# Order of the expert quads in a one-core hybrid SSD / convolution / hierarchical-MoE block

## The chip, the core and the metric

The kernel runs on one core of a Trainium2 chip. The metric is the device time of one execution in microseconds; of several executions the median is given.

## What is computed

One decoder layer over 512 tokens of width 1024: a gated SSD branch and a causal convolution branch, an output projection, then a hierarchical mixture of experts, a gate from per-layer embeddings and a final norm. The change touches the mixture of experts alone. Cut to that, the reference is:

```python
g_idx = argmax(u @ wg + bg)                      # one group of 4 for each token
top_v, top_i = top_k(e_logits[g_idx], 2)         # two of the 8 experts in it
gate_w = softmax(top_v) * g_prob
hdn = silu(xb @ w_gate[e]) * (xb @ w_up[e])      # for each of 32 experts e, on its tokens
out[token] += (hdn @ w_down[e]) * gate_w
```

Each expert has three float32 matrices of 1024x512 or 512x1024, 2 MiB each. All 32 experts are computed, so 192 MiB of expert weights are read in every execution.

## The kernel before

**Slots and quads.** The 32 experts are put into 32 slots. A slot holds 32, 64 or 96 tokens; the most loaded experts get the widest slots (NFIX and RANK, lines 51 to 67; the first four slots belong to experts 0 to 3, whatever their load). A quad is four strips of 32 tokens, 128 in all: "22" is a quad of two experts with two strips each, "31" two experts with three strips and one, "211" three experts. PLAN (line 52) lists the quads, one string for each group; a group of two quads shares a dispatch and a combine. Tokens over a slot's width would be handled by a loop behind the groups (line 1704), as often as the routing of the tokens needs.

**Units.** Each quad makes six units (lines 1351 to 1369): four of `gu_unit` (gate and up, two halves each) and two of `d_unit`. A unit multiplies 32 times: on each of 32 steps one strip of tokens (128x32, the stationary operand) against 512 columns of that strip's expert weights. So every unit has 32 matmuls, in whatever way the four strips fall to experts. A unit loads one piece of 1 MiB for each expert of its quad (lines 1209 and 1222): two pieces in a "22" or "31" quad, three in a "211" quad.

**The weight queue.** `pump` (lines 270 to 283) issues the loads in the order of the units on SP's queue, while there is room: ten pages of 1 MiB hold expert pieces. When a unit's matmuls have been issued, its pages are given back (line 369), and on the chip the next loads wait until TensorE has finished with them. For the experts behind the first four, SP first reads the expert's number (line 1182), which the router has worked out.

**Other work of TensorE between the units.** `step` runs one unit and `after` (lines 341 to 353) then inserts tasks: `disp` (line 1280, gathers the tokens of the next group by one-hot matmuls, four tasks for each group), `back` (line 1286, one for each quad) and `combine` (line 1317, adds the outputs of the group before to the tokens, eight for each group). What decides is a credit: a unit adds 1.27 for each half MiB that it loaded less 3.5 of its own, up to 5; a task takes its cost off; tasks go in while the credit is above zero, or once their due unit is reached (`task`, lines 1364, 1377, 1383). A hidden-layer step stands between a quad's fourth and fifth unit (`hid_act`, `hid_mul`, `hid_tr`, lines 1224 to 1241). `hot` (line 1248) builds the one-hot tables of the next group on VectorE, one instruction for each expert.

In the rows, `w<-eg`, `w<-eu` and `w<-ed` are the loads of gate, up and down weights; `acc<-w,cj` is a matmul of a gate or up unit, `acc<-w,m` of a down unit, `acc<-w,uh` and `acc<-w,ul` of `disp`, `acc<-identr,w` and `acc<-cb,w` of `back`, and `acc` from `ct`, `btok`, `k`, `bt` with `glu` of `combine`. Line 120 and line 282 are helpers that issue all of these.

Of the kernel before, what the change touches and what calls it, by code (L numbers as in the profile page):

```python
# [48 lines left out]


NFIX = 4
PLAN = ["22 22", "22 211", "31 211", "22 211", "31 211", "22 211", "211"]
GROUPS = []
CAP = []
for _g in PLAN:
    GROUPS.append([])
# [1852 lines left out]
```

## Time and profile before

| | |
|---|---|
| median of 3 runs | 1097.81 us (1093.88, 1097.98, 1097.81) |
| the profiled execution, its own time | 1095.38 us |
| its span | 1093.7 us, mean granted clock 0.981 |
| busy in the span | PE 93%, PEld 61%, DVE 51%, ACT 32%, POOL 1% |
| expert units | from 544 us to 1026 us of the span |
| DMA queue of SP | 252.73 MB in 94896 packets, 61.0% of the 16 engines' span |

Times in the rows are microseconds from the start of the span. The last group (one "211" quad, with the projection of the layer embeddings) is followed by the gate of the layer embeddings and the final norm, from 1034 us to the end.

### The profile page before, as it was taken

How to read it: one execution, taken by the hardware profiler on the slowest of the kernel's cores; microseconds unless marked ns; L12 is line 12 of the kernel's file. 1: busy time of each engine (PE TensorE's matmuls, PEld its weight loads, DVE VectorE, ACT ScalarE, POOL GpSimd, SP SyncE). 2: the span in 40 equal slices, each digit the busy share in tenths (PEclk: the TensorE clock that was granted, in tenths of full speed). 3: DMA queues.
4: the chain of work that ended last, by engine and by line, in shares of the span. 5: the costliest groups of instructions: out<-in, count | busy, mean ns of one | idle time of the engine just before them, and what ended most of it. 6: DMA issues, size and time to landing. Idle time of an engine off the chain costs nothing. (4 is left out here: it accounts for less than half of the span.)

```text
span 1093.7 us, 15677 instructions
## 1 busy us (share of the span) xinstructions
PE 1013.0 (93%) x6262; PEld 669.4 (61%) x6262; DVE 561.5 (51%) x1004; ACT 344.7 (32%) x646; POOL 14.7 (1%) x32
## 2 busy tenths in 40 slices
PE   5999999999989999999799998988979979889796
PEld 4788889877767887788634453433513515345485
DVE  6689998897889975653621311202103102022465
ACT  6433446776443234423411020110100100121263
POOL 1000000000000000000000000000000000000010
PEclk9999999999999999999899999999999999999899
DMA  9423222201323323456199999999999999999701
GB/s 269 108 65 104 81 79 77 78 1 40 89 66 95 98 80 117 145 194 229 39 369 393 375 380 422 421 421 421 420 420 420 421 422 421 417 407 376 304 2 77
DMA packets 95660, 255.97 MB, mean 234 GB/s; under 512 B 4784, under 2 KB 62144, under 8 KB 71008
## 3 DMA queue, kind: packets, MB, share of 16 engines
q1 hardware_dynamic: 94896, 252.73, 61.0%
q0 software_dynamic: 688, 2.22, 0.8%
q8 instruction: 50, 0.82, 0.3%
q14 instruction: 26, 0.21, 0.1%
HBM read 252.83 MB, written 2.10 MB: 233 GB/s over the span
## 5 line engine op out<-in xcount | busy, mean ns | idle before, releaser
L120 PE MATMUL acc<-uh,w 128*128 128x512 f32 x704 | 230.9, 400 | 2.4 <-DVE w L120 1.6
L120 PE MATMUL acc<-w,cj 128*32 128x512 f32 x1664 | 202.4, 603 | 15.8 <-DMA w<-eu 9.5
L120 PE MATMUL acc<-w,uh 128*128 128x256 f32 (+2 forms) x752 | 161.9, 325 | 0.9 <-DVE w L120 0.9
L120 PEld LDWEIGHTS acc<-uh,w 128*128 128x128 f32 x704 | 132.2, 188 | 33.4 <-DVE w L120 2.6
L120 PE MATMUL acc<-w,m 128*32 128x512 f32 (+1 forms) x960 | 129.3, 582 | 15.5 <-DMA w<-ed 10.5
L120 PEld LDWEIGHTS acc<-w,cj 128*32 128x32 f32 x1664 | 54.3, 111 | 141.9 <-issue 109.5
L120 PE MATMUL acc<-ul,w 128*128 128x512 f32 x352 | 137.4, 390 | 0.0
L120 DVE SCALAR_TENSOR_TENSOR cj<-glu,chan,cj 128x512 f32<-128x512 f32 x180 | 130.9, 748 | 2.2
L120 PEld LDWEIGHTS acc<-w,uh 128*128 128x128 f32 x752 | 118.7, 193 | 21.0 <-issue 10.2
L120 DVE TENSOR_TENSOR w<-w 128x1024 fp32r<-128x1024 f32 x86 | 104.6, 1221 | 32.3 <-ACT w L302 32.0
L120 PE MATMUL acc<-w,ul 128*128 128x256 f32 (+2 forms) x488 | 117.0, 306 | 0.0
L302 ACT CAST w<-w 128x1024 fp32r<-128x1024 f32 x86 | 89.5, 1052 | 55.3 <-PE acc L120 49.7
L120 PE MATMUL acc<-w 128*128 128x512 f32 x384 | 100.3, 399 | 3.1 <-ACT w L302 2.4
L120 DVE TENSOR_TENSOR k<-k,acc 128x512 f32<-128x512 f32 x21 | 19.2, 912 | 154.0 <-PE acc L120 154.0
L120 PEld LDWEIGHTS acc<-w,m 128*32 128x32 f32 (+1 forms) x960 | 43.4, 124 | 85.1 <-issue 51.9
L120 DVE TENSOR_TENSOR Z<-Z,acc 128x512 f32<-128x512 f32 x64 | 43.4, 686 | 86.5 <-PE acc L120 86.5
L120 PEld LDWEIGHTS acc<-w 128*128 128x128 f32 x384 | 72.6, 191 | 21.7 <-ACT w L302 2.8
L120 PEld LDWEIGHTS acc<-w,ul 128*128 128x128 f32 x488 | 77.1, 189 | 5.5
L120 PEld LDWEIGHTS acc<-ul,w 128*128 128x128 f32 x352 | 66.2, 188 | 15.0 <-issue 1.7
L1226 ACT ACTIVATE k<-acc 128x512 f32<-128x512 f32 x13 | 7.8, 598 | 164.1 <-PE acc L120 164.1
L120 DVE SCALAR_TENSOR_TENSOR bt<-glu,chan,bt 128x512 f32<-128x512 f32 x60 | 43.0, 749 | 0.7
L1277 ACT COPY cj<-acc 128x512 f32<-128x512 f32 (+1 forms) x28 | 15.6, 556 | 82.0 <-PE acc L120 82.0
(270 smaller groups left out, 876.3 us busy)
## 6 DMA issues: line engine op xcount, KB each, us to landing
w<-eg SPq DMA_DIRECT2D x64, 1024.0 KB, 14.1
w<-eu SPq DMA_DIRECT2D x64, 1024.0 KB, 15.1
w<-ed SPq DMA_DIRECT2D x64, 1024.0 KB, 15.2
w<-w_in SPq DMA_DIRECT2D x52, 512.0 KB, 5.1
w<-w_ssd_out SPq DMA_DIRECT2D x8, 512.0 KB, 4.7
w<-w_conf_out SPq DMA_DIRECT2D x8, 512.0 KB, 4.3
w<-w_o SPq DMA_DIRECT2D x8, 512.0 KB, 4.5
w<-w_ple_gate SPq DMA_DIRECT2D x8, 512.0 KB, 13.3
```

The source lines that it names most:

```text
L120: return f(*a, **k)
L302: nc.scalar.copy(u["wh"], u["raw"])
L1226: nc.scalar.activation(t, PG.pop((gi, q, 0)), AF.Silu)
L1277: nc.scalar.copy(t, pt[:, :2 * w].rearrange("p (k s) -> p k s", k=2))
```

## The change

PLAN is written in another order. Before and after there are five "22" quads, two "31" quads and six "211" quads, and the groups 0, 5 and 6 are the same. Group 1 was "22 211" and becomes "211 211"; group 2 was "31 211" and becomes "31 22"; group 3 was "22 211" and becomes "31 211"; group 4 was "31 211" and becomes "22 211".

```diff
 NFIX = 4
-PLAN = ["22 22", "22 211", "31 211", "22 211", "31 211", "22 211", "211"]
+PLAN = ["22 22", "211 211", "31 22", "31 211", "22 211", "22 211", "211"]
 GROUPS = []
```

GROUPS, CAP and RANK are derived from PLAN, and so are the constants `rank`, `cap` and `cap0` that the router uses. The loads, units and tasks follow from GROUPS by the code described above.

## Rows read from the trace of the kernel before

**Rows 1.** The page, 40 slices: granted clock and DMA rate
```profile
PEclk9999999999999999999899999999999999999899
...
GB/s 269 108 65 104 81 79 77 78 1 40 89 66 95 98 80 117 145 194 229 39 369 393 375 380 422 421 421 421 420 420 420 421 422 421 417 407 376 304 2 77
```

**Rows 2.** Busy time by stretch; last columns: granted clock, DMA share, GB/s
```profile
572.00:600.00 28.00, 27.22 (x248) 13.40 (x244) 4.01 (x8) 4.81 (x8) 0.00 (x0) 1.00 0.98 394
600.00:605.00 5.00, 5.00 (x52) 1.43 (x44) 0.32 (x1) 0.84 (x2) 0.00 (x0) 1.00 0.92 323
605.00:660.00 55.00, 53.87 (x444) 26.03 (x436) 12.86 (x27) 7.11 (x12) 0.00 (x0) 1.00 0.98 387
660.00:960.00 300.00, 270.14 (x2042) 117.57 (x2046) 51.11 (x106) 32.97 (x56) 0.76 (x1) 0.98 1.01 420
```

**Rows 3.** Waits of SP's queue, 605 to 660 us
```profile
SPq L282 <- PE acc L120: 40.6, 12, 6.8
```

**Rows 4.** Issues of weight loads on SP in order of time
```profile
574.88 4.47 SPq L282 DMA_DIRECT2D w<-ed  x4
581.74 1.54 SPq L282 DMA_DIRECT2D w<-eg  x2
585.18 0.90 SPq L282 DMA_DIRECT2D w<-eu  x2
594.41 0.91 SPq L282 DMA_DIRECT2D w<-eg  x2
601.35 1.27 SPq L282 DMA_DIRECT2D w<-eu  x2
604.78 4.34 SPq L282 DMA_DIRECT2D w<-ed  x4
616.63 5.95 SPq L282 DMA_DIRECT2D w<-eg  x3
```

**Rows 5.** TensorE in order of time, groups 0 and 1
```profile
563.16 5.34 PE L120 MATMUL acc<-w,m 128*32 128x512 f32 x32
...
569.79 0.64 PE L120 MATMUL acc<-identr,w 128*128 128x128 f32 x4
...
571.21 3.64 PE L120 MATMUL acc<-w,m 128*32 128x512 f32 x32
574.67 10.48 PE L120 MATMUL acc<-w,cj 128*32 128x512 f32 x96
585.08 1.20 PE L120 MATMUL acc<-w,uh 128*128 128x256 f32 x8
...
590.74 3.64 PE L120 MATMUL acc<-w,cj 128*32 128x512 f32 x32
...
604.57 3.62 PE L120 MATMUL acc<-w,cj 128*32 128x512 f32 x32
608.12 0.50 PE L120 MATMUL acc<-ct,glu 128*128 128x512 f32 x1
...
612.97 3.64 PE L120 MATMUL acc<-w,cj 128*32 128x512 f32 x32
```

**Rows 6.** Loads of the down weights: nanoseconds of an issue, then issue to landing
```profile
L282 SPq DMA_DIRECT2D w<-ed x64: 327/333/1303, 512.7 to 1007.2; - x64
...
DMA to landing us min/median/max: 4.9/15.2/21.3
```

**Rows 7.** Waits of TensorE, 660 to 960 us
```profile
PE acc L120 <- DMA w<-eu: 9.5, 8, 1.4
```

**Rows 8.** Busy time by stretch, after the three-expert quad of group 1
```profile
660.00:665.00 5.00, 4.13 (x22) 1.17 (x26) 0.09 (x1) 0.59 (x1) 0.00 (x0) 0.73 1.02 428
...
675.00:695.00 20.00, 19.94 (x138) 9.29 (x142) 7.14 (x14) 0.60 (x1) 0.00 (x0) 1.00 1.01 420
```

**Rows 9.** VectorE in order of time: one-hot tables of group 1, and the next instruction
```profile
576.33 1.49 DVE L120 TENSOR_TENSOR w<-prev,prev 128x256 fp32r<-128x256 f32 x5
594.54 1.10 DVE L120 TENSOR_TENSOR k<-k,acc 128x512 f32<-128x512 f32 x1 [16.72 <-PE acc L120]
```

**Rows 10.** TensorE, the last down unit of the last group
```profile
1022.37 3.62 PE L120 MATMUL acc<-w,m 128*32 128x512 f32 x26 [1.48 <-DMA w<-ed]
```

## Prediction

> **What bounds the kernel now.** I read the page's forty slices first. From 570 us to about 980 us the DMA rate is flat near 420 GB/s, except in the first slices, which show 369, 393, 375 and 380 [rows 1]. The busy time by stretch puts numbers to this: 420 GB/s as a mean over the 300 us from 660, but only 387 from 605 to 660 and 323 from 600 to 605 [rows 2]. Where the rate is flat, the weight stream sets the pace, and TensorE waits for weights [rows 7]. Where it is lower, TensorE is busy almost without a break (53.87 of 55 us) [rows 2], and SP's queue waits for TensorE to give pages back [rows 3]. So the expert stage has two bounds, one after the other. Until some point in group 1 it is TensorE that decides when the next load starts; from there to the last group it is the DMA rate. The last down unit still waits for its weights [rows 10], so a microsecond in which the stream stands still before 660 us comes out at the end.
>
> At 420 GB/s a piece of 1 MiB (1.049 MB) takes 2.50 us. A unit of three pieces thus wants 7.5 us of stream, one of two pieces 5.0 us. TensorE's own time for a unit is the same for both: 32 matmuls, 3.6 us with what follows at once, 10.41 us for three in a row from 574.67 to 585.08, so 3.5 us each [rows 5].
>
> **The change, part by part.** *Work.* The same 13 quads, 78 units, 192 pieces, tasks and slot widths are there in another order. The slots sorted by width are the same list, so the same token counts meet the same widths, and what overflows does not change. Matmuls, bytes and issues are equal: 0 us by itself.
>
> *Group 0* keeps its quads. Its pages and units up to 604.57 us, where group 1 starts on TensorE [rows 5], stay; the losses before 605 stay too. 32 pieces had been issued just after 601.35 and two more followed at 604.78, before the first unit of group 1 ended at 608.1 [rows 4, 5]. After the change these are the same 34 pieces by count, of other experts.
>
> *Group 1, first quad: two pieces become three for each unit.* This is the only place where I see the time move. Now each unit frees two pages, and between units TensorE does five combines from 608.12 to 612.97 (0.97 us each), three more behind the next units, then dispatches of 1.9 us (three from 585.08 to 590.74) and a back of 1.4 us (569.79 to 571.21) [rows 5]. Two pages are 5.0 us of stream, while TensorE needs more than that from one unit to the next, so the stream stops. After the change a unit frees three pages, 7.5 us of stream. I follow it by hand. The 31st to 34th piece were issued from 601.35 on; with about 2 us of start (a load on an empty queue lands after 4.9 us [rows 6], of which 2.5 are transfer) the stream is fed until 603.4 + 4 × 2.5 = 613.4. The first unit ends at 608.1 and frees three pages: fed until 620.9. The credit after a three-piece unit rises by 6 × 1.27 − 3.5 = 4.1 instead of 1.6, so six combines follow instead of five; the second unit ends at 608.1 + 5.8 + 3.6 = 617.5, in time by 3.4 us: fed until 628.4. Two combines, third unit at 623.0: fed until 635.9. The fourth unit at 626.6: until 643.4. Then four dispatches (now two here and two later) and the hidden step, some 8 us, fifth unit at 638.1, two backs, sixth unit at 644.5; the stream is ahead by 5 to 6 us at its narrowest there, and then gains 4 us a unit. So nothing of the loss after 605 us should be left in group 1, and from the second quad's third unit on TensorE waits for weights.
>
> The loss that goes: (420 − 387)/420 × 55 us = 4.3 us [rows 2]. The margins of 3.4 us and more, less 2 us of start, could be off by a page; I bound what is left between 0 and 1 us and take 0.1. No gain beyond 600 us is possible in this place, since all before is the same: with the loss from 600 to 605, (420 − 323)/420 × 5 = 1.2 us, the upper bound is 5.5 us.
>
> *Groups 2 and 3.* Three quads of two experts now follow each other ("31", "22", "31"), where a three-expert quad stood between. Their stream is 36 × 2.5 = 90 us. TensorE's work in the same stretch: 18 units × 3.5 = 63; 16 combines × 0.97 = 15.5; six dispatches × 1.9 = 11.4; four backs × 1.4 = 5.6; three hidden steps and a slow start of a down unit (5.34 instead of 3.64 [rows 5]) about 5. That is 100.5 us, so the stream's lead shrinks by 10.5 us. Its lead at the start is what is queued: pieces land 15.2 us after their issue in the median, 21.3 at most [rows 6]. Between 5 and 11 us are left, where 2 are needed. I bound the loss between 0 and 2 us; the nearest row, a single two-expert quad after a three-expert one, runs at 420 GB/s with TensorE 19.94 of 20 us busy [rows 8]. I take 0.2. What is late next is the weight stream itself, whose lead comes back in group 3's "211".
>
> *VectorE, SP.* Group 1 has six one-hot tables instead of five; five take 1.49 us, and the next instruction finds VectorE idle for 16.72 us [rows 9]. Without that cover it would cost 0.3 us. SP reads six expert numbers instead of five for group 1 and fewer for group 2; with an issue of 0.33 us [rows 6] against 2.5 us of stream it stays ahead. 0 us.
>
> *The hardware's rate.* The whole sum rests on 420 GB/s [rows 2]. The Trainium skill, page DMA: Bandwidth & Descriptors, section Where 436 GB/s comes from, says that for loads from HBM about 358 GB/s bind. By that, a piece would take 2.93 us and the stream would have been the bound before 605 us already, so the change would give nothing. The trace differs from it; the same page has a single-core measurement of 425 GB/s, which the row is near.
>
> **Sum.** 4.3 − 0.1 − 0.2 = 4.0 us less. The profiled execution took 1095.38 us, 1.7 more than its span; it would become 1091.4. It lies 2.4 us under the median shown and inside the runs, 1093.88 to 1097.98. Carried to the median: 1097.81 − 4.0 = 1093.8 us.
>
> **Rivals.** *No gain.* The stream could stop elsewhere for as long: TensorE in groups 2 and 3 could use up the lead and give back 2 to 4 us. For it: the sum of 100.5 against 90. Against it: the lead of 15 us or more. It gives 1096 to 1098.5 us. Chance 0.17.
>
> *More than the stretch shows.* All loss after 600 us goes, and the issue in threes keeps the stream fuller: 5.5 us and a little more, 1091 to 1092. The 300 us at 420 leave nothing further to take. Chance 0.10.
>
> *Slower, by the clock.* In group 1 nearly the whole second quad now waits for weights, and TensorE's clock falls in such waits: the granted clock is 0.73 just after the present three-expert quad's waits, and 1.00 in the quad behind it [rows 8]. If it stayed at the lower of its two levels (1.2 GHz instead of 2.4) through the first quad of group 2, six units and eight combines would take twice as long: 6 × 3.5 + 7.8 = 29 us more. The lead takes 5 to 11 of them, and the gain 4: slower by 14 to 20 us, about 1115. The place decides as soon as that quad's units take more than about 5 us each. Against it stands the row behind the waits, 1.00. The Trainium skill, page TensorE: Matmul & The Clock Gate, section HAM oscillation, describes just such bursts between waits for DMA that start at the low clock each time; by that rule alone the waiting quad would run slow under its own waits, which costs nothing there. Chance 0.04.
>
> **How the numbers follow.** My forecast, 2 to 5.5 us less, has the remaining 0.69. A measurement of this kernel can tell about 0.5% (5.5 us) from no change; the runs before lie 4.1 us apart, which is as much as the effect. So the forecast lies mostly inside "same", with part of its chance beyond the line. Faster by over 0.5%: 0.30 (the larger rival and some 0.2 of the forecast, by the spread of the runs). Same: 0.65. Slower: 0.05. The range: from the lowest run less most of the upper bound, 1093.88 − 4.9 = 1089.0, to the highest run with no gain, 1098.5.
>
> **What would show it.** Right: 415 GB/s or more from 605 to 660 us; waits of SP's queue for TensorE there that no longer empty the stream; TensorE waiting for weights before 660 us in group 1's second quad; group 1 ending later than now, by some 11 us (six more pieces less the loss), and group 2 shorter; the last down unit about 4 us earlier, and the part behind it as long as now. Wrong: a rate under 415 GB/s in groups 2 or 3, where the lead ran out; a granted clock under 0.9 through group 2's first quad; a last down unit at 1022 us as before.

## The result and the profile after

The changed kernel takes 1090.26 us in the median of four runs (1089.99 to 1092.18), the kernel before 1097.89 in four (1093.88 to 1098.13). The ratio is 0.9949, with a 95% interval of 0.9928 to 0.9969: faster by 0.51%, just past the 0.5% at which the prediction draws its line between "same" and "faster". The two medians lie 7.6 us apart, the ratio stands for 5.6 us; with four runs of each I go by the ratio and its interval, 3.4 to 7.9 us. The profiled execution took 1089.99 us with a span of 1088.3, 5.4 less than before. The stretch from 605 to 660 us is where the two traces part.

The page of the changed kernel, granted clock and DMA rate in forty slices, as in [rows 1]:

```profile
PEclk9999999999999999999899998999999999999898
...
GB/s 267 94 75 89 106 78 78 79 1 39 78 78 78 116 78 116 122 162 270 59 315 416 400 422 420 421 420 421 410 414 420 421 421 422 416 418 391 299 2 77
```

The flat part now begins three slices earlier (416, 400, 422 stand where 393, 375, 380 stood), and has a shallow dent of its own (410, 414). The busy time by stretch of the changed kernel, columns as in [rows 2]:

```profile
572.00:600.00 28.00, 27.22 (x244) 13.39 (x240) 4.07 (x9) 4.80 (x8) 0.00 (x0) 1.00 1.01 415
600.00:605.00 5.00, 5.00 (x52) 1.56 (x48) 0.52 (x1) 1.04 (x2) 0.00 (x0) 1.00 0.82 303
605.00:660.00 55.00, 51.08 (x398) 25.24 (x394) 11.65 (x25) 6.31 (x11) 0.00 (x0) 0.97 1.01 421
660.00:960.00 300.00, 273.68 (x2112) 122.48 (x2108) 53.74 (x108) 34.60 (x59) 0.76 (x1) 0.98 1.01 419
...
780.00:795.00 15.00, 15.00 (x132) 8.82 (x132) 2.65 (x10) 3.61 (x6) 0.00 (x0) 1.00 0.98 388
```

Between 605 and 660 us the stream has its full rate, 421 GB/s instead of 387. TensorE is no longer busy throughout: 3.9 of 55 us are idle. The waits of SP's queue in the same stretch, beside [rows 3], show the new bound:

```profile
SPq L282 <- PE acc L120: 33.2, 10, 9.2
SPq L282 <- DMA w<-eg: 3.0, 2, 1.9
SPq L282 <- DMA w<-eu: 0.4, 1, 0.4
```

SP still waits 33 us for TensorE. That is no loss, since the stream keeps its 421 GB/s through these waits, so enough loads are under way. A wait of the issuing queue says nothing by itself; the rate beside it decides. The issues of the changed kernel in order of time, beside [rows 4], now come in threes from group 1 on:

```profile
574.97 4.03 SPq L282 DMA_DIRECT2D w<-ed  x3
581.41 3.77 SPq L282 DMA_DIRECT2D w<-eg  x3
585.42 9.79 SPq L282 DMA_DIRECT2D w<-eu  x3
601.14 3.77 SPq L282 DMA_DIRECT2D w<-eg  x3
605.15 3.77 SPq L282 DMA_DIRECT2D w<-eu  x3
609.16 15.45 SPq L282 DMA_DIRECT2D w<-ed  x6
```

TensorE in order of time through group 1 of the changed kernel, combines left out, beside [rows 5]:

```profile
604.37 3.62 PE L120 MATMUL acc<-w,cj 128*32 128x512 f32 x32
...
613.71 3.64 PE L120 MATMUL acc<-w,cj 128*32 128x512 f32 x32
...
619.33 7.07 PE L120 MATMUL acc<-w,cj 128*32 128x512 f32 x64
...
634.27 3.64 PE L120 MATMUL acc<-w,m 128*32 128x512 f32 x32
...
640.62 3.64 PE L120 MATMUL acc<-w,m 128*32 128x512 f32 x32
644.08 4.47 PE L120 MATMUL acc<-w,cj 128*32 128x512 f32 x38
649.72 3.63 PE L120 MATMUL acc<-w,cj 128*32 128x512 f32 x30 [1.17 <-DMA w<-eu]
```

The first unit starts at 604.37 (604.57 before). The six units of the first quad end at 608.0, 617.4, about 622.9, 626.4, 637.9 and 644.3 us. In the second quad's second unit TensorE waits for weights for the first time. The end of the expert stage, beside [rows 10]:

```profile
1016.99 3.62 PE L120 MATMUL acc<-w,m 128*32 128x512 f32 x26 [1.49 <-DMA w<-ed]
```

The last down unit waits for its weights as before, and comes 5.4 us earlier; the span ends 5.4 us earlier. What lies behind the experts costs what it did.

### The profile page after: what moved, and what is told of

The parts are those of the page before. It is cut to its first block, busy times and chain, and to the rows that moved or that the text cites. A ratio compares the mean times of both kernels' runs of the same rounds, so it can differ in the third digit from the quotient of the medians.

```text
span 1088.3 us, 15678 instructions
## 1 busy us (share of the span) xinstructions
PE 1010.9 (93%) x6262; PEld 673.1 (62%) x6262; DVE 561.3 (52%) x1004; ACT 344.5 (32%) x646; POOL 14.7 (1%) x32
## 5 line engine op out<-in xcount | busy, mean ns | idle before, releaser
L120 PE MATMUL acc<-w,cj 128*32 128x512 f32 x1664 | 199.5, 603 | 16.2 <-DMA w<-eg 8.5
L120 PE MATMUL acc<-w,m 128*32 128x512 f32 (+1 forms) x960 | 126.5, 582 | 12.3 <-DMA w<-ed 7.6
```

Of the source, the lines that this page charges most:

```text
L120: return f(*a, **k)
```

## Experiments

The theory to be tested, A: in group 1's first quad a two-piece unit frees 5.0 us of stream while TensorE needs more than that to the next unit, so the stream runs dry; three pieces keep it full. Beside it stood a question on the dent at 780 us, whether a lower mean rate is lost time (C) or not, because the pace is set by the slowest of the 16 DMA engines (D). In all runs "the changed kernel" is the one predicted.

**The changed kernel again.** No edit.

> The changed kernel once more, as the measure for the other runs of this call. Every theory: 4 to 8 us under the kernel before, 415 GB/s or more from 605 to 660 us, about 390 from 780 to 795 us.

Measured: 1091.16 us against 1095.73 for the kernel before in the same session, ratio 0.9959 (0.9940 to 0.9979). By stretch:

```profile
605.00:660.00 55.00, 51.26 (x398) 25.11 (x393) 10.82 (x24) 5.98 (x10) 0.00 (x0) 0.97 1.01 422
780.00:795.00 15.00, 15.00 (x136) 8.65 (x139) 2.65 (x10) 3.61 (x6) 0.00 (x0) 1.00 0.98 386
```

Both marks of the change repeat.

**The first quad alone.** The order before, with the quads of group 1 exchanged:

```diff
-PLAN = ["22 22", "22 211", "31 211", "22 211", "31 211", "22 211", "211"]
+PLAN = ["22 22", "211 22", "31 211", "22 211", "31 211", "22 211", "211"]
```

> The order before with only the two quads of group 1 exchanged (211 first, then 22). Theory A (the stream ran dry because a two-piece unit frees too little weight for the time that TensorE needs in group 1's first quad): the first quad alone decides, so the 605 to 660 us stretch runs at 415 GB/s or more and the time is 4 to 6 us under the kernel before, within 1.5 us of the changed kernel. Rival B (two three-expert quads in a row are needed, as the quad behind the first one would run dry in its turn): 380 to 400 GB/s in that stretch and at most 2 us under the kernel before.

Measured: 1090.6 us, ratio 0.9939 (0.9920 to 0.9958). By stretch:

```profile
605.00:660.00 55.00, 54.14 (x444) 26.18 (x436) 12.10 (x27) 7.03 (x12) 0.00 (x0) 1.00 1.01 420
```

TensorE is as busy here as in the kernel before (54.14 of 55 us), and still the stream is full. So one three-expert quad at this place does all of it; B falls. The second three-expert quad in group 1 and the new order of groups 2 to 4 bring nothing that can be measured (1091.16 us for the changed kernel in the same session).

**TensorE's work taken out instead.** Both kernels without the eight combines of group 0, whose result, the outputs of experts 0 to 3, is thus not added:

```diff
-        for n in range(2):
+        for n in range(2 if gi else 0):
             for c in range(NT):
                 task(u + 1, u + 5, 0.23 * 2 * len(g), combine, gi, c, n)
```

> The kernel before without the eight combines of group 0 (the outputs of experts 0 to 3 are not added). That takes 7.8 us of TensorE out of group 1's first quad, and no load. Theory A: the stream no longer runs dry there, 410 GB/s or more from 605 to 660 us, 3.5 to 6 us under the kernel before, as much as the change brings. Rival (TensorE's work counts in full in the expert stage): 7 to 8 us under it.

Measured: 1090.62 us against 1095.15, ratio 0.9955 (0.9940 to 0.9970). By stretch:

```profile
605.00:660.00 55.00, 51.36 (x430) 21.77 (x426) 7.01 (x19) 7.24 (x13) 0.00 (x0) 0.97 1.01 421
```

> The changed kernel without the eight combines of group 0, as in the run before. Theory A: the stream is already full there, so 7.8 us less TensorE work bring 0 to 1 us against the changed kernel, and the two kernels without these combines lie within 1.5 us of each other. Rival: 7 to 8 us under the changed kernel.

Measured: 1090.99 us, ratio 0.9952 (0.9934 to 0.9970). By stretch:

```profile
605.00:660.00 55.00, 47.93 (x376) 20.24 (x368) 5.72 (x16) 5.98 (x10) 0.00 (x0) 0.97 1.01 422
```

This pair is the clearest. The same 7.8 us of TensorE work is worth about 4.5 us in the kernel before, as much as the change brings (4.6 and 5.8 us in the medians of two other sessions), and nothing that shows in the changed kernel (which had no run beside this pair; it took 1091.16 and 1091.12 us elsewhere). Either remedy fills the stream (421 and 421 GB/s), and the second one on top finds nothing left to fill; TensorE just waits longer (47.93 us busy). The rival, that TensorE's work counts in full, falls.

**No run of three two-expert quads.** The changed order, groups 2 and 3 rearranged:

```diff
-PLAN = ["22 22", "211 211", "31 22", "31 211", "22 211", "22 211", "211"]
+PLAN = ["22 22", "211 211", "31 22", "211 31", "22 211", "22 211", "211"]
```

> The changed order, but no three two-expert quads in a row (31 22, then 211 31, where it was 31 22, then 31 211). Theory C (the pace is the mean rate of the stream, each GB/s lost is time lost): the 1.1 us lost from 780 to 795 us come back, 1 to 1.5 us under the changed kernel. Rival D (the pace is the slowest of the 16 DMA engines, which goes on working while the stream thins out): no dip in the rate, but no gain either, within 0.6 us of the changed kernel, and the first and the last of a load's 16 arrivals 5 to 6 us apart before the last group, as in the kernel before, instead of 3.

> The order without three two-expert quads in a row once more, to tell theory C from rival D. C: 1 to 1.5 us under the changed kernel of this call in the median and in the last down unit of group 5. D: within 0.6 us of it in both.

Beside them the changed kernel a third time, in the second session:

> The changed kernel beside the next run, on one chip. 0.994 to 0.997 of the kernel before; last down unit of group 5 at 966.5 to 968 us.

Measured, first session: 1090.9 us against 1091.16 for the changed kernel; second: 1091.52 against 1091.12 (ratios 0.9943, 0.9959; 0.9949, 0.9945, each with about 0.002 to either side). The rearranged order has no dent (420 and 423 GB/s from 780 to 795 us). The medians differ by less than 0.5 us, once each way, where C wanted 1 to 1.5 less; but such a comparison tells only 1.5 to 2 us apart (see the last experiment), so the times alone leave C open. The ends of the profiles would have misled: the last down unit of group 5 began at 966.02 us in the first profile of the rearranged order and at 969.32 in the second. The third profile of the changed kernel has no dent at all, by stretch:

```profile
605.00:660.00 55.00, 50.85 (x408) 25.16 (x400) 11.04 (x24) 5.98 (x10) 0.00 (x0) 1.00 1.01 421
...
780.00:795.00 15.00, 15.00 (x140) 7.78 (x132) 2.20 (x7) 3.02 (x5) 0.00 (x0) 1.00 1.01 421
```

and its last down unit of group 5:

```profile
966.80 3.62 PE L120 MATMUL acc<-w,m 128*32 128x512 f32 x26 [1.46 <-DMA w<-ed]
```

That is 966.80 without the dent and 967.25 and 967.32 us with it.

The completion records of the loads decide it. A weight load leaves 16 of them on its semaphore, spread over some microseconds, and TensorE waits for the last one (in one of the profiles below it came at 973.66 us, and the waiting unit began at 973.70). I take the time from the 89th weight load to the 151st, each end a mean over the eight loads from there, worked out from the records. By the mean of a load's 16 records it is 156.1 and 156.2 us in the two profiles with the dent, 155.0 in the three without (the changed kernel's third and both of the rearranged order). By the last record it is 155.7 and 155.5 us with the dent, and 155.6, 155.7 and 155.7 without. So the dent delays the mean arrival by 1.1 to 1.2 us, just what the rate says, and the last arrival, for which TensorE waits, by nothing that shows. The lead does run nearly out where three two-expert quads follow each other, in some executions, and it costs nothing here. C falls, and D's account fits: its mark, arrivals 5 to 6 us apart without a dent instead of 3, came out at 4.7 and 4.8 us in the rearranged order and 4.9 in the changed kernel's third profile, against 2.6 and 2.5 in the two with the dent (means from 860 to 960 us).

**The dip without the gain.** Group 1 as before, three two-expert quads in a row behind it:

```diff
-PLAN = ["22 22", "22 211", "31 211", "22 211", "31 211", "22 211", "211"]
+PLAN = ["22 22", "22 211", "31 22", "31 211", "22 211", "211 211", "211"]
```

> Group 1 as before (22 211), but three two-expert quads in a row behind (31 22, then 31 211), and 211 211 as group 5. Theory A: the loss from 605 to 660 us stays, 385 to 390 GB/s. Theory C: another 1.1 us is lost where the stream thins out, 1 us over the kernel before. Rival D: the dip lets the slow engine catch up, so the time is that of the kernel before or up to 2 us under it.

Measured: 1096.71 us, ratio 1.0005 (0.9992 to 1.0018). By stretch:

```profile
605.00:660.00 55.00, 53.73 (x443) 26.12 (x436) 12.45 (x25) 6.59 (x12) 0.00 (x0) 1.00 0.97 386
660.00:960.00 300.00, 270.36 (x2047) 119.59 (x2045) 51.19 (x106) 33.08 (x56) 0.76 (x1) 0.98 1.01 421
```

A holds: with the old group 1 the loss stays, whatever follows. No dip formed in this profile (421 GB/s through 300 us), so it says nothing on C against D.

**A small load on few engines, and on all.** The changed kernel with 12 extra loads between the weight loads, 17 rows of 256 floats, or 16 rows of 272, into a tile that nobody reads:

```diff
+        if u["plain"] and n >= NB + 22 and (n - NB) % 4 == 2 and n < NB + 70:
+            if "x" not in state:
+                state["x"] = st([128, 512], F32, "cj", 9)
+            nc.sync.dma_start(state["x"][:17, :256], cst[:17, :256])
```

> The changed kernel with 12 extra small loads between the weight loads of groups 1 to 5, of 17 rows of 1 KiB each (17 KiB), of data that nobody reads; a row count of 17 is meant to put a load on few of the DMA engines. Theory C: 0.21 MB more in 200 MB, 0.5 us and 12 issues, under 1 us slower than the changed kernel. Rival D: each holds one engine for 0.6 to 1.1 us, so 6 to 13 us slower, and the arrivals of one weight load drift apart by as much.

Measured: 1098.06 us, ratio 1.0023 (1.0012 to 1.0034), 7.1 us over the changed kernel without combines in the same session, which is as fast as the changed kernel elsewhere (1091.16 and 1091.12).

> The changed kernel with 12 extra loads of the same 17 KiB in the same places, but in 16 rows of 1088 bytes, so that all 16 engines share each. Both theories: under 1 us slower than the changed kernel; the arrivals of one weight load stay about 2 to 3 us apart. If it is as slow as the run with 17 rows, it is the extra load in SP's queue that costs, not one engine.

Measured: 1093.98 us, ratio 0.9989 (0.9977 to 1.0000), 3.0 us over it. The last down unit of group 5 with 17 rows, then with 16:

```profile
973.70 3.62 PE L120 MATMUL acc<-w,m 128*32 128x512 f32 x26 [1.43 <-DMA w<-ed]
```

```profile
969.92 3.62 PE L120 MATMUL acc<-w,m 128*32 128x512 f32 x26 [1.47 <-DMA w<-ed]
```

With 17 rows D's 6 to 13 us were met and C's "under 1 us" was not. With 16 rows both missed: an extra small load costs 0.25 us even when it is shared, not 0.04 us as its bytes would. Of the 7.1 us some 4 are left for the number of engines. The Trainium skill, page DMA: Bandwidth & Descriptors, section Why a DMA increments its semaphore by 16 and not by 1, says that the number of engines a load uses is the largest up to 16 that divides the slowest dimension of both its sides; by this rule one for 17 rows, 16 for 16 rows. The traces agree. SP's queue (packets, MB, share of the 16 engines' time) in the changed kernel, with 17 rows, then with 16:

```profile
q1 hardware_dynamic: 94896, 252.73, 60.9%
```

```profile
q1 hardware_dynamic: 95112, 252.93, 61.0%
```

```profile
q1 hardware_dynamic: 95280, 252.94, 61.0%
```

The 12 loads add 216 packets with 17 rows, 17 and one more for each load, and 384 with 16 rows, 16 and 16 more. And a load of 17 rows leaves two completion records, one about 0.45 us after its issue and one 13 to 19 us after it, where a load of 16 rows leaves 16. The records of the weight loads show where the 4 us lie. From the 37th weight load to the 161st (each end again a mean over eight) the mean record takes 312.5 us with 17 rows and 312.7 with 16; the last record takes 317.9 and 313.7, that is 4.2 us more. In the third profile of the changed kernel the two are 310.5 and 312.0. So the extra loads delay the mean arrival alike, and only the last one tells them apart, as D says. The 16 arrivals of a weight load drift apart by as much as 11.5 us with 17 rows. In the mean from 860 to 960 us they lie 8.4 us apart with 17 rows and 5.7 with 16, where 2 to 3 were expected, against 4.9 in that third profile.

**The kernel before against itself.**

> The kernel before against itself, for the resolution of the comparison and for a second profile of it. A ratio of 1.000 within 0.002; 385 to 390 GB/s from 605 to 660 us; the last down unit of group 5 within 1.5 us of 972.81 us.

Measured: ratio 0.9995 (0.9980 to 1.0010). By stretch, and the last down unit of group 5:

```profile
605.00:660.00 55.00, 53.46 (x436) 26.26 (x428) 11.95 (x26) 6.79 (x12) 0.00 (x0) 1.00 0.98 388
```

```profile
971.47 3.62 PE L120 MATMUL acc<-w,m 128*32 128x512 f32 x26 [2.54 <-DMA w<-ed]
```

One comparison thus tells 1.5 to 2 us apart, and two profiles of one kernel differ by 1.3 us at that place, where the first had

```profile
972.81 3.62 PE L120 MATMUL acc<-w,m 128*32 128x512 f32 x26 [1.45 <-DMA w<-ed]
```

The two of the rearranged order above lie 3.3 us apart there. The rate from 605 to 660 us is the steadier witness: 387, 386 and 388 with the old group 1 and all its combines, 420 to 422 in every other profile taken.

## Why the prediction was right

**The place and the mechanism** hold: the first quad of group 1, and the stream that runs dry there. The unit ends followed by hand (608.1, 617.5, 623.0, 626.6, 638.1, 644.5) were met within 0.3 us, so the credit rule was read rightly, with its six combines instead of five. TensorE's first wait for weights came one unit earlier than said. The hidden-layer step of group 1's second quad moved from 660.14 to 669.43 us, by 9.3 where the end of group 1 was to come some 11 later.

**The main term** was 4.3 us and measured (421 − 387)/421 × 55 = 4.4 us. Its remainder, put at 0.1, doesn't show.

**Groups 2 and 3**: 0.2 us was taken, with 2 as the bound. The stream did thin out at the place named, to 388 and 386 GB/s in two of three profiles, which is 1.2 us of rate and one of the prediction's own signs of being wrong (under 415 GB/s in groups 2 or 3). So less of the lead was left there than the 5 to 11 us worked out. That it cost nothing has a reason that the prediction didn't have: the last arrivals of the loads came no later for it. The small cost was right, partly by luck; the step's place was right, its lead was taken too long, and its assumption that rate lost is time lost failed.

**The sum** said 4.0 us; the profiled executions lie 5.4 apart. With the later profiles the last down unit of group 5 moves from 972.1 (mean of 972.81 and 971.47) to 967.1 us (mean of 967.25, 967.32, 966.80), by 5.0 us. The completion records show where: I compare the last record of the same weight load by number, as a mean over the three profiles with the old group 1 (the kernel before twice, and the dip without the gain) and over the three of the changed kernel. The changed kernel is 0.2 us ahead at the 35th load, at 617 us, 5.3 at the 45th, at 647 us, then 4.4 to 5.4 as far as the last load, where it is 4.7. So the gain is made in the first quad of group 1, and nothing behind it adds or takes more than profiles differ by. "The losses before 605 stay" held: 0.6 us at most from the 21st load to the 35th, and the rate from 572 to 600 us, 394 and 415 GB/s in the first two profiles, was 412 in the second profile of the kernel before, so that difference is spread. Of the 4.7 us 4.4 are the main term; the rest, and the 5.4 of the one pair, lie within what profiles of one kernel differ by.

**The number** was 1093.8 us and the median 1090.26. Of the 3.5 us between them 1.4 are the gain (5.4 less 4.0); the other 2.1 come from the step that carried the sum to the median of three runs, 1097.81. The kernel before had medians of 1095.73, 1095.15 and 1096.95 in later sessions with 18 and more runs; the profiled execution, 1095.38, was the better base. The sum against it, 1091.4, was off by 1.4 from the profiled execution after. On the prediction's own line of 0.5% the ratio falls on "faster", to which it gave 0.30, by a hundredth of a per cent; the interval, 0.31 to 0.72%, covers both sides.

**The rivals.** *No gain* falls with every run of the changed kernel; *slower, by the clock* too: the first quad of group 2 ran at a granted clock of 1.00 from 680 to 720 us though TensorE had waited before it and the clock had fallen to 0.72 (655 to 660 us) and 0.66 (670 to 675) between the waits, each a mean over its two levels. One reading behind that rival was off: the stretch with 0.73 in [rows 8], 660 to 665 us, lies inside the three-expert quad and not behind it, and the waits just before and in it are for VectorE and ScalarE in the hidden-layer step (1.27 and 0.73 us), not for weights. The case of *more than the stretch shows* is where the single ratio points (5.6 us), the repeats (4.6 and 5.8 us in the medians) lie on both sides of it.

**The rate.** The 358 GB/s that the Trainium skill names as one core's half of a memory stack's rate (page DMA: Bandwidth & Descriptors, section Where 436 GB/s comes from) would have made the change worth nothing. The trace of this one core differs: the stream ran at 419 to 422.

## What to carry to other kernels

Where a weight stream feeds TensorE through a fixed number of pages, compare for each stretch the stream time that one unit's pages hold with TensorE's time from one unit to the next, side work included. Put the units that carry the most bytes where the side work is densest and the stream's lead is smallest; behind that point the order was free here. Read the loss from the transfer rate of the stretch, not from the waits of the issuing queue; where the rate only dips, look at the last arrivals of the loads behind the dip, since 1.2 us of rate cost no time here. And take the base of a small forecast from more than three runs.

## What the runs showed of the hardware

Two things I had not expected. First, a load of 17 KiB between large ones cost 0.25 us when shared by all engines and 0.6 us (7.1/12) in 17 rows on one engine, 6 to 15 times the 0.04 us that its bytes take at 420 GB/s. Second, the arrivals of one 1 MiB load spread with time as long as the stream never pauses: from 2.8 us after 660 us to 4.4 after 771 and 6.0 after 919 us in the kernel before, and they fell from 3.5 back to 1.6 us through the dent of the changed kernel. Both of these steps fall on 16 KiB packets of the instruction queue, but they are two of 16 such packets between 660 and 960 us in that profile. One is in the stretch from 766 to 771 us (its DMA queues: packets, MB, share of the 16 engines' time):

```profile
q1 hardware_dynamic: 285, 2.07, 100.0%
q8 instruction: 1, 0.02, 1.4%
```

That a load counts by its last arrival and not by the mean rate is what the dent and the extra loads of 17 and 16 rows show. That an instruction packet is what holds up one engine would fit; it was not tried by itself and stays open.
